# Where the sums of a two-level block product run: VectorE or GpSimd, and who stores the hidden features

## The chip, the cores and the metric

The kernel runs on one core of a Trainium2 chip. The metric is device time in microseconds of one execution; the time before is the median of three executions, 3026.63 us (3024.52 to 3027.03). The profiler recorded one further execution, of 3015.44 us, and its span from first to last instruction is 3013.7 us. Clock readings in this document (for example "at 882.9") are microseconds from the start of that span.

The engines are named as in the profile: PE (matrix products), DVE (VectorE), ACT (ScalarE), POOL (GpSimd) and SP, whose queue starts DMA transfers. Each engine works through its own queue in order.

## The reference, cut to what matters

A two-layer decoder trunk on 1024 tokens of width 1024: a mixer, a cross-attention and an MLP in each layer, each wrapped in two norms. Only the MLP is touched by the change, so it stands here alone:

```python
def _sq_relu_mlp(hn, w1, w2):
    return jnp.square(jax.nn.relu(hn @ w1)) @ w2

# in reference(), for each of 2 layers, after the mixer and the cross-attention
f = _sq_relu_mlp(_rmsnorm(h, g_ffn_pre[layer]), ffn_w1[layer], ffn_w2[layer])
h = h + _rmsnorm(f, g_ffn_post[layer])
```

The hidden width is 4096. All data is fp32.

## The kernel before, in words

**Products of fp32 in three parts.** Every fp32 operand is split into a high part (rounded by ACT, `split`, L137) and a low part (the remainder, on DVE, L143). A product then takes three matmuls: high by high, high by low, low by high (`prod`, L552 to L558). In the profile's rows `wh` and `wl` are the two parts of a weight or feature block, `hnh` and `hnl` those of the tokens.

**Seven products in place of eight.** The MLP's matrices are cut into 2 x 2 blocks, and a block product is made from seven smaller products by a Strassen-like scheme. The seven are numbered and run in the order `SEVEN = (1, 2, 6, 5, 7, 3, 4)`. Products 1 and 2 use blocks as they are, and so do 3 and 4 on one side; the others use sums of blocks. The hidden width is cut into eight groups (`GROUPS`), so *product (g, p)* is product p of group g: 24 matmuls of 128 x 128 by 128 x 512 each, in *up* (tokens by w1) as in *down* (hidden by w2).

**Up.** `up(g, p)` (L575) takes the next weight from a stream that makes weights up to three products ahead (`Stream`, its `ahead`). Making a weight means loading a block (`unit`, L474), forming its sum where the product needs one (`seven`, L479, four sums for each group, on POOL, rows of L489 in the profile), and splitting it. The tokens' blocks are made once for each layer: the last tiles of the cross-attention are normed, turned by PE (rows of `tp`) and copied by ACT into four blocks b11, b12, b21, b22 (`transpose_blocks`), and `sum_blocks` (L247) makes t2, t1, t3 and t4 from them and splits all of these and b22. It is one call, between `up(1, 1)` and `up(1, 2)`; four of its eight sums are on DVE (L260, L261) and four on POOL (L266, L272). Products 1 and 2 of groups 0 and 1 are run first, since they need no sum of the tokens, and the other ten products of these two groups after them.

**Evacuation.** Products 1, 6 and 5 are copied out of PSUM by ACT (`keep`, L587). Products 2, 7 and 3 go to `hidden` (L564): DVE adds the kept part (L571), then DVE makes the squared ReLU in one instruction (L572), and SP stores the result to DRAM (`hd`, L573). Product 4 has nothing to add: ACT makes the ReLU, DVE the square (L569). The same SP queue carries the loads of blocks.

**Down.** The first seven groups run in chunks (0, 1), (2, 3), (4, 5), (6). For product p both groups of a chunk follow each other: (0, 1), (1, 1), (0, 2), (1, 2), (0, 6) and so on. Both operands, the hidden blocks (read back from `hd`) and the blocks of w2, are made two products ahead: a block is loaded when a product first asks for it, so at p = 6 the load, two sums on each side (on POOL), and the splits all come in a row. Group 7 is done at the end without the scheme.

**What sets the order.** A scheduler puts each engine's instructions in an order by its own timeline; the order in which Python issues them sets priorities. Buffers (34 units of 4 KB a partition, 12 weight buffers, 3 raw ones) decide when a load can start.

Of the kernel before, what the change touches and what calls it, by code (L numbers as in the profile page):

```python
# [45 lines left out]
def half_cols(half):  # L46
    return slice(half * HALF, half * HALF + HALF)
# [30 lines left out]
class Trunk:  # L78
# [168 lines left out]
    def sum_blocks(self):  # L247

        nc, B, parts = self.nc, self.blocks, self.bparts
        sub, dve, pool = ALU.subtract, nc.vector, nc.gpsimd  # L250

        def part(name, xs, lo_eng="dve"):
            parts[name] = [self.parts([P, 2, HALF], "hn") for _ in range(2)]
            for w, x in zip(parts[name], xs):
                self.split(*w, x, lo_eng=lo_eng)

        b11, b12, b21, b22 = (B[n] for n in BLOCKS)
        t2 = [self.u([P, 2, HALF], F32, "blk") for _ in range(2)]
        for q in range(2):
            dve.tensor_tensor(b11[q], b12[q], b11[q], sub)  # L260
            dve.tensor_tensor(t2[q], b22[q], b11[q], sub)  # L261
        part("t2", t2)
        part("t1", b11)
        del B["11"], b11
        for q in range(2):
            pool.tensor_tensor(b12[q], b22[q], b12[q], sub)  # L266
        part("t3", b12)
        del B["12"], b12
        part("22", b22)
        del B["22"], b22  # L270
        for q in range(2):
            pool.tensor_tensor(b21[q], b21[q], t2[q], sub)  # L272
        del t2
        part("t4", b21)
        del B["21"], b21

    def norm_pre(self, h, gpre, hn=None):
# [200 lines left out]

    def seven(self, p, st, load, new, make, signs, eng):  # L479

# [46 lines left out]
    def up_weights(self, l):  # L527
        nc, st = self.nc, {}

        def make(gp):  # L530
# [4 lines left out]

            x = self.seven(p, st.setdefault(g, {}), load, lambda: self.wt([P, 2, HALF], F32, "sum"), None, 1, nc.gpsimd)
            w = self.parts([P, 2, HALF], "w", self.wt)
# [8 lines left out]
    def ffn(self, l):  # L546
# [13 lines left out]
        with self.psum(8, 0):  # L560
# [3 lines left out]
            def hidden(c, ps, g, b, q):  # L564

                x = self.t2()
                if c is None:
                    nc.scalar.activation(x, ps, AF.Relu)
                    nc.vector.tensor_tensor(x, x, x, ALU.mult)  # L569
                else:  # L570
                    nc.vector.tensor_tensor(x, c, ps, ALU.add)  # L571
                    nc.vector.scalar_tensor_tensor(x, x, 0.0, x, ALU.max, ALU.mult)  # L572
                nc.sync.dma_start(hd[g][BLOCKS.index(b), :, half_cols(q)], x)  # L573

            def up(g, p):  # L575
# [20 lines left out]
                for n in {2: ("b", 1), 7: (5,), 3: ("c", 6), 4: ("a",)}.get(p, ()):  # L596
                    del G[n]

            up(0, 1)
            self.flush(1)  # L600
            up(0, 2)
            self.flush()
            up(1, 1)
            self.sum_blocks()
            up(1, 2)
            for g in range(2):
                for p in SEVEN[2:]:
                    up(g, p)
            for g in range(2, GROUPS):
# [13 lines left out]

        sts = {}

        def make(gp):
            g, p = gp
            sa, sb = sts.setdefault(g, ({}, {}))
            res = []
            for st, load, sign in ((sa, hid(g), 1), (sb, second(g), -1)):  # L630
                x = self.seven(p, st, load, lambda: self.u([P, 2, HALF], F32, "blk"), None, sign, nc.gpsimd)
                w = self.parts([P, 2, HALF], "w", self.wt)
                self.split(*w, x)
                res.append(w)
            return res

        with self.psum(8, 0):
            W = Stream(self, [(g, p) for ch in CHUNKS for p in SEVEN for g in ch], 2, make=make)
            for ch in CHUNKS:
# [1286 lines left out]
```

## Time and profile before

| What | Value |
|---|---|
| median of 3 executions | 3026.63 us |
| the profiled execution, its span | 3015.44 us, 3013.7 us |
| mean granted PE clock | 0.977 |
| DVE, ACT, POOL busy, share of the span | 66%, 42%, 40% |
| up of layer 0, of layer 1, start of the first product | 870.86, 2331.51 |
| down of layer 0, of layer 1, start of the first product | 1208.79, 2669.91 |
| DMA moved | 385.09 MB, mean 128 GB/s |

How to read the rows that follow in the document. A row of the timeline has the start, the duration, the engine, the line of the kernel, the operation, what it writes and reads, and how many like it in a row (x); in square brackets stands how long the engine was idle before it and which instruction ended that. A row of the windows has a stretch of the span, its length, and for each engine the time in which it was busy and the number of instructions; behind them the granted PE clock, the DMA share and GB/s. A row of the waits has who waited for whom, the sum, the number of times and the longest. Where several instructions overlap at their ends, the durations of a row are a little longer than the distance between starts.

### The profile page before, as it was taken

The page shows a single profiled execution, that of the slowest core. Times are in us where ns is not written, and L with a number is a line of the kernel's source. Part 1 is how long each engine was busy: PE and PEld are TensorE (multiplying, and loading weights), DVE is VectorE, ACT ScalarE, POOL GpSimd, SP SyncE. Part 2 cuts the span into 40 slices and gives each one's busy share as a digit, 9 for nine tenths or more (in the row PEclk, how much of TensorE's full clock was granted, in tenths as well). Part 3 has the DMA queues.
Part 4 walks back from the last instruction along what each step waited for, and adds up shares of the span by engine and source line. Part 5 has one row for each costly group of instructions (what it writes and reads, how often), then busy time and mean ns, then how long its engine had stood idle before and what let it go on. Part 6 is the DMA issues. An engine that isn't in the chain of part 4 may idle for free. (4 is left out here: it accounts for less than half of the span.)

```text
span 3013.7 us, 38030 instructions
## 1 busy us (share of the span) xinstructions
PE 2843.7 (94%) x14470; PEld 2356.3 (78%) x14470; DVE 2000.8 (66%) x2372; ACT 1279.1 (42%) x2167; POOL 1205.0 (40%) x778
## 2 busy tenths in 40 slices
PE   7998999999998999799999998988999799989998
PEld 6787888787876888688867888987788588867886
DVE  5237778764367555599876657888634855548995
ACT  4445666543343323333345565553433333224332
POOL 2205544243344331776050113357433533347733
PEclk9999999999998999899999999999999899999999
DMA  4264444451322334432153346556223132253303
GB/s 164 103 179 131 156 155 146 137 187 42 117 102 85 101 110 151 164 111 85 64 203 109 117 144 193 182 171 237 84 91 112 67 111 103 105 207 108 105 28 140
DMA packets 165223, 385.09 MB, mean 128 GB/s; under 512 B 16748, under 2 KB 66316, under 8 KB 165040
## 3 DMA queue, kind: packets, MB, share of 16 engines
q1 hardware_dynamic: 165040, 382.66, 37.7%
q8 instruction: 114, 1.87, 0.3%
q14 instruction: 69, 0.57, 0.1%
HBM read 267.86 MB, written 113.69 MB: 127 GB/s over the span
## 5 line engine op out<-in xcount | busy, mean ns | idle before, releaser
L143 DVE TENSOR_TENSOR wl<-blk,wh 128x1024 fp32r<-128x1024 f32 x276 | 482.5, 1771 | 255.1 <-ACT wh L137 253.4
L489 POOL TENSOR_TENSOR blk<-blk 128x1024 f32<-128x1024 f32 x128 | 387.9, 3053 | 251.6 <-DMA blk<-hd 124.1
L137 ACT ACTIVATE wh<-blk 128x1024 fp32r<-128x1024 f32 x276 | 282.6, 1056 | 405.8 <-PE op L557 191.9
L556 PE MATMUL up<-hnh,wh 128*128 128x512 f32 x896 | 356.9, 399 | 16.3 <-ACT keep L587 9.2
L557 PE MATMUL up<-hnl,wh 128*128 128x512 f32 x896 | 356.9, 398 | 6.0 <-DVE hnl L143 6.0
L558 PE MATMUL up<-hnh,wl 128*128 128x512 f32 x896 | 354.6, 396 | 0.0
L556 PE MATMUL op<-wh 128*128 128x512 f32 x784 | 306.2, 394 | 27.5 <-ACT wh L137 27.5
L557 PE MATMUL op<-wl,wh 128*128 128x512 f32 x784 | 308.8, 394 | 4.8 <-DVE wl L143 4.7
L558 PE MATMUL op<-wh,wl 128*128 128x512 f32 x784 | 307.5, 392 | 0.0
L143 POOL TENSOR_TENSOR wl<-raw,wh 128x1024 fp32r<-128x1024 f32 x66 | 158.7, 2416 | 223.9 <-ACT wh L137 208.5
L137 ACT ACTIVATE wh<-raw 128x1024 fp32r<-128x1024 f32 (+1 forms) x163 | 170.6, 1058 | 129.8 <-DMA raw<-hd 25.4
L556 PEld LDWEIGHTS up<-hnh,wh 128*128 128x128 f32 x896 | 170.7, 191 | 59.3 <-ACT keep L587 10.7
L557 PEld LDWEIGHTS up<-hnl,wh 128*128 128x128 f32 x896 | 170.4, 190 | 46.2 <-DVE hnl L143 6.9
L558 PEld LDWEIGHTS up<-hnh,wl 128*128 128x128 f32 x896 | 169.8, 190 | 40.0
L143 DVE TENSOR_TENSOR wl<-raw,wh 128x1024 fp32r<-128x1024 f32 (+1 forms) x97 | 130.3, 1354 | 100.7 <-ACT wh L137 100.2
L556 PEld LDWEIGHTS op<-wh 128*128 128x128 f32 x784 | 148.8, 190 | 60.4 <-ACT wh L137 29.2
L187 POOL TENSOR_SCALAR st<-st 128x1 f32<-128x1 f32 x99 | 41.7, 421 | 358.8 <-ACT hn L299 306.6
L557 PEld LDWEIGHTS op<-wl,wh 128*128 128x128 f32 x784 | 149.0, 190 | 39.0 <-DVE wl L143 7.8
L489 POOL TENSOR_TENSOR sum<-blk 128x1024 f32<-128x1024 f32 x16 | 43.1, 2696 | 337.2 <-PE up L557 337.2
L558 PEld LDWEIGHTS op<-wh,wl 128*128 128x128 f32 x784 | 148.9, 190 | 30.4
L302 POOL TENSOR_TENSOR h<-h,hn 128x1024 f32<-128x1024 f32 x47 | 128.4, 2731 | 33.9 <-DVE hn L301 25.8
L587 ACT ACTIVATE keep<-up 128x512 f32<-128x512 f32 x96 | 56.7, 594 | 196.9 <-PE up L558 184.5
(439 smaller groups left out, 7200.0 us busy)
## 6 DMA issues: line engine op xcount, KB each, us to landing
blk<-in_ffn_w_dram SPq DMA_DIRECT2D x120, 512.0 KB, 3.9
h<-h SPq DMA_DIRECT2D x80, 512.0 KB, 4.0
hd<-t SPq DMA_DIRECT2D x128, 256.0 KB, 2.0
blk<-hd SPq DMA_DIRECT2D x56, 512.0 KB, 4.5
raw<-in_w_in_dram SPq DMA_DIRECT2D x24, 512.0 KB, 4.1
h<-in_x_dram SPq DMA_DIRECT2D x16, 512.0 KB, 7.0
raw<-in_xa_w_k_dram SPq DMA_DIRECT2D x16, 512.0 KB, 3.7
raw<-in_xa_w_v_dram SPq DMA_DIRECT2D x16, 512.0 KB, 3.9
```

The lines of the kernel that those rows point to most:

```text
L137: nc.scalar.activation(hi, src, AF.Copy)
L143: e.tensor_tensor(lo, src, hi.bitcast(F32), ALU.subtract)
L187: self.nc.gpsimd.tensor_scalar(dst, src, EPS, None, ALU.add)
L302: nc.gpsimd.tensor_tensor(h, h, t, ALU.add)
L489: eng.tensor_tensor(out, a, b, op)
L556: mm(ps, lh, rh, start=start and not i, stop=False, skip_group_check=True)
L557: mm(ps, lh, rl, start=False, stop=False, skip_group_check=True)
L558: mm(ps, ll, rh, start=False, stop=i == n - 1, skip_group_check=True)
L587: nc.scalar.activation(keep[:, q, :], ps, AF.Copy)
```

## The change

Five edits, all in the MLP:

1. In up, the four sums of weight blocks for each group move from POOL to DVE.
2. `sum_blocks` has all eight sums on DVE and becomes a generator of four steps: t2 and t1; t3; b22; t4. The first step is issued ahead of `up(1, 1)`, the second ahead of `up(1, 2)`, the others ahead of products 6 and 5 of group 0. The weight stream is two products ahead instead of three until `up(1, 2)` has been issued, then three.
3. `hidden` makes the squared ReLU on ACT in two instructions (ReLU, then Square) and stores it from ACT's own DMA queue. DVE keeps the add. For product 4 nothing is left on DVE.
4. In down, the blocks that the next product needs first are loaded one step earlier (`seq[n:n + 2]`).
5. In down, the sums of the first chunk (groups 0 and 1) move from POOL to DVE; the other chunks keep POOL.

```diff
     def sum_blocks(self):
...
-        sub, dve, pool = ALU.subtract, nc.vector, nc.gpsimd
+        tt = self.nc.vector.tensor_tensor
...
-            dve.tensor_tensor(b11[q], b12[q], b11[q], sub)
-            dve.tensor_tensor(t2[q], b22[q], b11[q], sub)
+            tt(b11[q], b12[q], b11[q], ALU.subtract)
+            tt(t2[q], b22[q], b11[q], ALU.subtract)
         part("t2", t2)
         part("t1", b11)
         del B["11"], b11
+        yield True
         for q in range(2):
-            pool.tensor_tensor(b12[q], b22[q], b12[q], sub)
+            tt(b12[q], b22[q], b12[q], ALU.subtract)
...
-            x = self.seven(p, st.setdefault(g, {}), load, lambda: self.wt([P, 2, HALF], F32, "sum"), None, 1, nc.gpsimd)
+            x = self.seven(p, st.setdefault(g, {}), load, lambda: self.wt([P, 2, HALF], F32, "sum"), 1, nc.vector)
...
                 x = self.t2()
-                if c is None:
-                    nc.scalar.activation(x, ps, AF.Relu)
-                    nc.vector.tensor_tensor(x, x, x, ALU.mult)
-                else:
+                if c is not None:
                     nc.vector.tensor_tensor(x, c, ps, ALU.add)
-                    nc.vector.scalar_tensor_tensor(x, x, 0.0, x, ALU.max, ALU.mult)
-                nc.sync.dma_start(hd[g][BLOCKS.index(b), :, half_cols(q)], x)
+                nc.scalar.activation(x, ps if c is None else x, AF.Relu)
+                nc.scalar.activation(x, x, AF.Square)
+                nc.scalar.dma_start(hd[g][BLOCKS.index(b), :, half_cols(q)], x)
...
+            W.ahead = 2
             up(0, 1)
             self.flush(1)
             up(0, 2)
             self.flush()
+            sums = self.sum_blocks()
+            next(sums)
             up(1, 1)
-            self.sum_blocks()
+            next(sums)
             up(1, 2)
+            W.ahead = 3
             for g in range(2):
                 for p in SEVEN[2:]:
+                    next(sums, None)
                     up(g, p)
...
+        seq = [(g, p) for ch in CHUNKS for p in SEVEN for g in ch]
+
+        def make(n):
+
+            for g, p in seq[n:n + 2]:
+                sa, sb = sts.setdefault(g, ({}, {}))
+                for st, load, more in ((sa, hid(g), {1: ("11",), 2: ("12",), 6: ("21", "22")}), (sb, second(g), {1: ("11",), 2: ("21",), 6: ("12", "22")})):
+                    for b in more.get(p, ()):
+                        if b not in st:
+                            st[b] = load(b)
...
-                x = self.seven(p, st, load, lambda: self.u([P, 2, HALF], F32, "blk"), None, sign, nc.gpsimd)
+                x = self.seven(p, st, load, lambda: self.u([P, 2, HALF], F32, "blk"), sign, nc.vector if g in CHUNKS[0] else nc.gpsimd)
```

How the instructions move is best seen at three places. A number behind a name tells one buffer from another; the two programs number differently.

**POOL where up begins, layer 0.** `h_8266` is the last token tile of the cross-attention, `st_8279` the norm factor of that tile; L489 is a sum of weight blocks. Before:

```order
L302 TENSOR_TENSOR h_8266<-h_8266,hn_8265 128x1024
L489 TENSOR_TENSOR sum_8346<-blk_8347,blk_8349 128x1024
L187 TENSOR_SCALAR st_8279<-st_8279 128x1
L489 TENSOR_TENSOR sum_8352<-sum_8346,blk_8232 128x1024
L489 TENSOR_TENSOR blk_8347<-blk_8232,blk_8347 128x1024
L188 TENSOR_TENSOR st_8279<-st_8279,mhalf_79 128x1
L489 TENSOR_TENSOR blk_8238<-blk_8238,sum_8352 128x1024
L266 TENSOR_TENSOR blk_8150<-blk_8159,blk_8150 128x1024
```

And now, with the first rows of down behind them:

```order
L306 TENSOR_TENSOR h_8266<-h_8266,hn_8265 128x1024
L187 TENSOR_SCALAR st_8279<-st_8279 128x1
L188 TENSOR_TENSOR st_8279<-st_8279,mhalf_79 128x1
L493 TENSOR_TENSOR blk_11141<-blk_11085,blk_11087 128x1024
L493 TENSOR_TENSOR blk_11143<-blk_11141,blk_10928 128x1024
```

The two small instructions of the norm have no sum ahead of them or between them any more, and POOL has nothing else in all of up.

**DVE where up's sums are made, layer 0.** `blk_7794` and `blk_7795` are the halves of b11, which become t1; t2 is `blk_8439`, `blk_8440` before and `blk_8396`, `blk_8397` now; `hnl` is a low part of a token block, `wl` of a weight. Before:

```order
L143 TENSOR_TENSOR wl_8530<-blk_8238,wh_8529 128x1024
L260 TENSOR_TENSOR blk_7794<-blk_8150,blk_7794 128x1024
L260 TENSOR_TENSOR blk_7795<-blk_8151,blk_7795 128x1024
L261 TENSOR_TENSOR blk_8439<-blk_8159,blk_7794 128x1024
L261 TENSOR_TENSOR blk_8440<-blk_8160,blk_7795 128x1024
L143 TENSOR_TENSOR wl_8561<-blk_8349,wh_8560 128x1024
L143 TENSOR_TENSOR hnl_8446<-blk_8439,hnh_8445 128x1024
L571 TENSOR_TENSOR t2_8508<-keep_8412,up_8494 128x512
L143 TENSOR_TENSOR hnl_8448<-blk_8440,hnh_8447 128x1024
```

Now the part from the first of these sums to the first low half of t2 reads:

```order
L260 TENSOR_TENSOR blk_7794<-blk_8150,blk_7794 128x1024
L260 TENSOR_TENSOR blk_7795<-blk_8151,blk_7795 128x1024
L143 TENSOR_TENSOR wl_8470<-sum_8418,wh_8469 128x1024
L143 TENSOR_TENSOR wl_8519<-blk_8419,wh_8518 128x1024
L261 TENSOR_TENSOR blk_8396<-blk_8159,blk_7794 128x1024
L267 TENSOR_TENSOR blk_8150<-blk_8159,blk_8150 128x1024
L261 TENSOR_TENSOR blk_8397<-blk_8160,blk_7795 128x1024
L267 TENSOR_TENSOR blk_8151<-blk_8160,blk_8151 128x1024
L143 TENSOR_TENSOR wl_8524<-blk_8238,wh_8523 128x1024
L143 TENSOR_TENSOR wl_8565<-blk_8421,wh_8564 128x1024
L275 TENSOR_TENSOR blk_7811<-blk_7811,blk_8396 128x1024
L143 TENSOR_TENSOR hnl_8403<-blk_8396,hnh_8402 128x1024
```

Ahead of these twelve now stand, in this order, the last tile's norm (L287), the split of the weight of (1, 2), the four sums of group 0's weights with two adds of `hidden` among them, and one more split: eight instructions from the split of (1, 2) on. So twenty instructions run from that split to the first low half of t2, and the second low half comes three further on.

**DVE where down begins, layer 0.** `acc` is the output's accumulator, `op` a PSUM bank. Before, with all sums on POOL:

```order
L143 TENSOR_TENSOR wl_10484<-blk_10481,wh_10483 128x1024
L143 TENSOR_TENSOR wl_10490<-blk_10487,wh_10489 128x1024
L658 TENSOR_TENSOR acc_10517<-acc_10517,op_10529 128x512
L658 TENSOR_TENSOR acc_10520<-acc_10520,op_10530 128x512
L658 TENSOR_TENSOR acc_10523<-acc_10523,op_10531 128x512
L143 TENSOR_TENSOR wl_10542<-blk_10539,wh_10541 128x1024
L658 TENSOR_TENSOR acc_10526<-acc_10526,op_10532 128x512
L143 TENSOR_TENSOR wl_10554<-blk_10549,wh_10553 128x1024
```

Now, from the sixth instruction behind the same two splits (there named `wl_10542` and `wl_10546`) to the last split of (0, 6); the five ahead of it are sums:

```order
L143 TENSOR_TENSOR wl_10602<-blk_10599,wh_10601 128x1024
L493 TENSOR_TENSOR blk_10607<-blk_10539,blk_10605 128x1024
L493 TENSOR_TENSOR blk_10637<-blk_10589,blk_10591 128x1024
L493 TENSOR_TENSOR blk_10537<-blk_10539,blk_10537 128x1024
L673 TENSOR_TENSOR acc_10573<-acc_10573,op_10585 128x512
L673 TENSOR_TENSOR acc_10576<-acc_10576,op_10586 128x512
L673 TENSOR_TENSOR acc_10579<-acc_10579,op_10587 128x512
L493 TENSOR_TENSOR blk_10487<-blk_10487,blk_10607 128x1024
L673 TENSOR_TENSOR acc_10582<-acc_10582,op_10588 128x512
L143 TENSOR_TENSOR wl_10610<-blk_10607,wh_10609 128x1024
```

Behind them follow four sums, a split, three sums and the split `wl_10650` that product (1, 6) needs. All sixteen sums of the first chunk are in DVE's queue among the splits, and the adds to `acc`, which wait for PE, stand among them.

More of the change, by code (lines that the diff above doesn't have):

```diff
@@ L247, in sum_blocks, with part @@
     def sum_blocks(self):
-        nc, B, parts = self.nc, self.blocks, self.bparts
-        sub, dve, pool = ALU.subtract, nc.vector, nc.gpsimd
-        def part(name, xs, lo_eng="dve"):
+        B, parts = self.blocks, self.bparts
+        tt = self.nc.vector.tensor_tensor
+        def part(name, xs):
             parts[name] = [self.parts([P, 2, HALF], "hn") for _ in range(2)]
             for w, x in zip(parts[name], xs):
-                self.split(*w, x, lo_eng=lo_eng)
+                self.split(*w, x)
         b11, b12, b21, b22 = (B[n] for n in BLOCKS)
@@ L264, in sum_blocks @@
         del B["11"], b11
+        yield True
         for q in range(2):
-            pool.tensor_tensor(b12[q], b22[q], b12[q], sub)
+            tt(b12[q], b22[q], b12[q], ALU.subtract)
         part("t3", b12)
         del B["12"], b12
+        yield True
         part("22", b22)
         del B["22"], b22
+        yield True
         for q in range(2):
-            pool.tensor_tensor(b21[q], b21[q], t2[q], sub)
+            tt(b21[q], b21[q], t2[q], ALU.subtract)
         del t2
@@ L275, in sum_blocks @@
         del B["21"], b21
+        yield True
     def norm_pre(self, h, gpre, hn=None):
@@ L477, in unit, with seven @@
         return t
-    def seven(self, p, st, load, new, make, signs, eng):
+    def seven(self, p, st, load, new, signs, eng):
         sub, add = ALU.subtract, ALU.add
@@ L624, in ffn @@
         sts = {}
-        def make(gp):
-            g, p = gp
-            sa, sb = sts.setdefault(g, ({}, {}))
+        seq = [(g, p) for ch in CHUNKS for p in SEVEN for g in ch]
[6 more added lines that the diff above has]
+                            st[b] = load(b)
+            g, p = seq[n]
+            sa, sb = sts[g]
             res = []
             for st, load, sign in ((sa, hid(g), 1), (sb, second(g), -1)):
-                x = self.seven(p, st, load, lambda: self.u([P, 2, HALF], F32, "blk"), None, sign, nc.gpsimd)
+                x = self.seven(p, st, load, lambda: self.u([P, 2, HALF], F32, "blk"), sign, nc.vector if g in CHUNKS[0] else nc.gpsimd)
                 w = self.parts([P, 2, HALF], "w", self.wt)
@@ L637, in ffn @@
         with self.psum(8, 0):
-            W = Stream(self, [(g, p) for ch in CHUNKS for p in SEVEN for g in ch], 2, make=make)
+            W = Stream(self, range(len(seq)), 2, make=make)
             for ch in CHUNKS:
```

## The prediction, made blind

> **What bounds the kernel now.** I read the page's first part, then the waits of PE, then windows over the MLP, and last the timelines of the engines around PE's idle times.
>
> ```profile
> PE 2843.7 (94%) x14470; PEld 2356.3 (78%) x14470; DVE 2000.8 (66%) x2372; ACT 1279.1 (42%) x2167; POOL 1205.0 (40%) x778
> ```
>
> PE is busy for 94% of the span, so an edit that moves work between the other engines can gain only where PE waits. The waits of PE between 840 and 1500, the MLP of layer 0, show where:
>
> ```profile
> PE op L556 <- ACT wh L137: 13.8, 2, 11.3
> PE tp L239 <- ACT wh L137: 7.4, 1, 7.4
> PE up L556 <- ACT keep L587: 4.6, 1, 4.6
> PE up L557 <- DVE hnl L143: 3.0, 1, 3.0
> PE up L556 <- ACT wh L137: 3.0, 1, 3.0
> PE op L557 <- DVE wl L143: 2.4, 2, 2.1
> ```
>
> A table of windows says what these cost. Its rows are the first nine products of up, the rest of up, the first six products of down and the 42 after them, then both starts in layer 1.
>
> ```profile
> 870.86:946.75 75.89, 57.85 (x233) 45.23 (x231) 64.37 (x45) 32.35 (x48) 46.88 (x19) 0.84 0.17 57
> 946.75:1208.79 262.04, 262.04 (x1133) 212.32 (x1132) 148.40 (x142) 79.24 (x101) 68.39 (x24) 1.00 0.35 121
> 1208.79:1262.59 53.80, 37.61 (x145) 29.41 (x144) 22.52 (x15) 15.68 (x20) 41.48 (x16) 0.84 0.48 177
> 1262.59:1491.07 228.48, 228.48 (x1009) 189.20 (x1008) 213.85 (x175) 91.19 (x95) 129.41 (x40) 1.00 0.24 78
> 2331.51:2407.77 76.26, 57.28 (x234) 45.12 (x231) 64.65 (x45) 32.12 (x48) 46.88 (x19) 0.87 0.16 57
> 2669.91:2723.53 53.62, 37.57 (x146) 29.29 (x145) 22.33 (x15) 15.69 (x20) 41.70 (x16) 0.84 0.49 179
> ```
>
> Past the starts PE is busy in every microsecond at full clock: 262.04 / 47 = 5.575 us for a product of up (0.232 a matmul), 228.48 / 42 = 5.44 for one of down (0.227). Nothing can be gained there. At the starts, nine products of up and two turns of token tiles (0.8 each) should take 51.8, and take 75.89: 24.1 lost, 24.5 in layer 1. Six products of down should take 32.6: 21.2 lost, 21.0 in layer 1. So **90.8 us** is all that this change can win. The idle time itself is 34.2 in a layer; the rest is a low clock (0.84 to 0.87) and slow matmuls behind it.
>
> **Up's start, part by part.** Timelines of POOL, DVE and PE around the first idle time:
>
> ```profile
> 872.56 0.21 POOL L187 TENSOR_SCALAR st<-st 128x1 f32<-128x1 f32 x1 [0.16 <-ACT hn L281]
> 872.86 0.56 POOL L188 TENSOR_TENSOR st<-st,mhalf 128x1 f32<-128x1 f32 x1
> 873.79 3.37 POOL L302 TENSOR_TENSOR h<-h,hn 128x1024 f32<-128x1024 f32 x1 [0.38 <-DVE hn L301]
> 877.12 3.38 POOL L489 TENSOR_TENSOR sum<-blk 128x1024 f32<-128x1024 f32 x1
> 880.58 0.22 POOL L187 TENSOR_SCALAR st<-st 128x1 f32<-128x1 f32 x1
> 880.88 2.40 POOL L489 TENSOR_TENSOR sum<-sum,blk 128x1024 f32<-128x1024 f32 x1
> 883.25 2.36 POOL L489 TENSOR_TENSOR blk<-blk 128x1024 f32<-128x1024 f32 x1
> 885.55 1.56 POOL L188 TENSOR_TENSOR st<-st,mhalf 128x1 f32<-128x1 f32 x1
> ```
>
> ```profile
> 887.15 3.35 DVE L283 SCALAR_TENSOR_TENSOR hn<-h,st,gain 128x1024 f32<-128x1024 f32 x1 [0.46 <-POOL st L188]
> 896.23 2.35 DVE L260 TENSOR_TENSOR blk<-blk 128x1024 f32<-128x1024 f32 x2
> ```
>
> ```profile
> 877.20 1.07 ACT L281 ACTIVATE hn<-h 128x1024 f32<-128x1024 f32 x1 [2.68 <-POOL h L302]
> 890.65 1.94 PE L239 MATMUL tp<-c_ident,hn 128*128 128x128 f32 x8 [7.37 <-ACT wh L137]
> ```
>
> The view puts the 7.37 down to a split, but the turn reads `hn`, which DVE ended at 890.5, because the norm factor of the last tile was stuck between sums on POOL. With the sums gone, the factor follows ACT's square: 878.4 + 0.9 (as at 872.56), DVE about 1.2, so 880.5. PE ends (0, 2) at 877.44 + 5.57 = 883.0, and this wait is **gone**. What is late next is t2. PE goes on with the turn, (1, 1) and (1, 2) and is through at 883.0 + 0.8 + 11.15 = 894.9. Product (0, 6) then needs t2's low halves, behind twenty instructions of DVE.
>
> ```profile
> 877.19 0.32 SPq L303 DMA_DIRECT2D h<-h  x1
> blk<-in_ffn_w_dram SPq DMA_DIRECT2D x120, 512.0 KB, 3.9
> L137 ACT ACTIVATE wh<-blk 128x1024 fp32r<-128x1024 f32 x276 | 282.6, 1056 | 405.8 <-PE op L557 191.9 <-PE up L557 82.5 <-POOL blk L489 81.4
> ```
>
> The first of the twenty splits the weight of (1, 2), whose load, made one product later now, sits on SP's queue behind the store of the last tile: 877.5 + 3.9 + 1.06 for ACT = 882.5. Eighteen of the twenty are of 128x1024; with POOL empty I take 2.35 / 2 = 1.18 each (the pair at 896.23), and two adds at 0.69 (the row at 1229.47 below). That is 22.6, so the first low half is there at 905.1 and the second, three on, at 908.6. PE does four high-by-high matmuls (0.9), which its new order puts first, meanwhile. It is idle for 905.1 - 894.9 - 0.9 = 9.3, works off twelve matmuls, and is idle 0.7 more. I add 1.5 for slow matmuls behind the idle time, from the turn that took 1.94 instead of 1.04. Loss 11.5 where it was 24.1: **12.6 won**. The bounds of one DVE sum are 1.18 and, if POOL shared the time with it as at 873.79, 3.4; POOL has no work there, so I take 1.18. From t3 on DVE leads PE by some 3 us for each product, so I cost the later waits (hnl 3.0, wh 3.0, keep 4.6) at nothing.
>
> **Down's start.** SP, POOL, ACT, DVE and PE, each from its timeline:
>
> ```profile
> 1198.82 13.25 SPq L573 DMA_DIRECT2D hd<-t  x6
> 1212.16 0.88 SPq L476 DMA_DIRECT2D blk<-hd  x2
> ```
>
> ```profile
> 1217.70 41.80 POOL L489 TENSOR_TENSOR blk<-blk 128x1024 f32<-128x1024 f32 x16 [53.03 <-DMA blk<-hd]
> 1214.26 2.01 ACT L137 ACTIVATE wh<-blk 128x1024 fp32r<-128x1024 f32 x2 [3.92 <-issue]
> 1215.36 2.36 DVE L143 TENSOR_TENSOR wl<-blk,wh 128x1024 fp32r<-128x1024 f32 x2 [3.64 <-ACT wh L137]
> 1229.47 0.69 DVE L658 TENSOR_TENSOR acc<-acc,op 128x512 f32<-128x512 f32 x1 [0.67 <-PE op L558]
> 1233.26 1.20 PE L556 MATMUL op<-wh 128*128 128x512 f32 x4 [2.54 <-ACT wh L137]
> 1254.96 2.08 PE L556 MATMUL op<-wh 128*128 128x512 f32 x4 [11.26 <-ACT wh L137]
> ```
>
> The loads for p = 6 stood behind six stores on SP, and the sixteen sums then took POOL 41.8. The stores leave SP, so the loads go out when buffers come free, and the inputs are there before 1217. That alone gains nothing: the sums now follow two splits that wait for the weight buffers of (0, 1), and end at 1217.7 as before. Nine instructions of 1.18 bring 1228.3; the third add waits for PE until 1230.2; a sum, an add and a split bring 1233.2. PE ended (1, 2) at 1230.6 and did four matmuls: idle 1.7. It ends (0, 6) at 1233.2 + 20 x 0.227 = 1237.7. Six further (7.1) and ACT's split give (1, 6) its operand at 1241.4: idle 3.7. PE does four matmuls, then waits for ACT's two splits of (0, 5) until 1243.5 (idle 1.2), does four more, and the rest of both, 40 matmuls, ends at 1253.5. Seven products without a wait would end at 1246.9: loss 6.6, with 1.5 for the clock 8.1, where it was 21.2. **13.1 won**. From there DVE leads again. The chunks behind keep POOL; I cost the earlier loads at nothing, since PE never waited there.
>
> **ACT and the stores.** In up's steady part ACT is busy 79.24 in 47 products, so 11.8 in a group of seven (39.0).
>
> ```profile
> L393 ACT ACTIVATE t<-t 128x512 f32<-128x512 f32 x40 | 25.0, 629 | 68.6 <-DVE t L392 68.5
> L571 DVE TENSOR_TENSOR t<-keep,up 128x512 f32<-128x512 f32 x96 | 65.2, 680 | 33.1 <-PE up L558 33.0
> hd<-t SPq DMA_DIRECT2D x128, 256.0 KB, 2.0
> ```
>
> A group adds eight squares and six ReLUs of 0.63, 8.8 in all, and eight stores. The trace shows no store issued by ACT; the bounds are nothing and SP's time to landing, 2.0, and I take 0.32, SP's issue. That makes 23.2 of 39.0: hidden under PE. The copies that free PSUM wait behind a ReLU for at most the two adds of a product (0.68 each), and PE comes back to a bank a whole product later. DVE loses six squares and two multiplies in a group and gains four sums, hidden too. A microsecond that is not hidden here counts fourteen times in a run (seven later groups, two layers).
>
> **The sum.** 12.6 + 13.1 = 25.7 a layer, 51.4 in two layers, so about 52: the profiled execution goes from 3015.4 to 2963, and the median, which lies 11.2 above it, from 3026.6 to **2975**.
>
> **What the Trainium skill adds.** The POOL sum at 873.79 and DVE's norm at 887.15 take 3.4 where 2.36 and 1.2 would do, so the two engines exclude each other. The Trainium skill, "SBUF — State Buffer", section "Who interferes with whom", says that a DVE instruction with two SBUF inputs contends with a GpSimd one that reads SBUF; the trace agrees (3.35). "Perfetto Trace Analysis" in the Trainium skill, section "Optimizing Scalar/DVE Operations", warns for this reason that moving work between those two might not help; rival A gives its time. The Trainium skill, "TensorE: Matmul & The Clock Gate", section "What's actually happening", lets the clock fall after an idle window of about 3.4 us. By that rule the four 1.5s would go, an estimate of 2969. The trace does not quite agree: four matmuls took 1.20 after 2.54 of idle, where 3 x 0.227 + 0.39 = 1.07 is usual.
>
> **The rivals.** *A: DVE gains nothing on POOL.* If each moved sum held DVE for POOL's 2.36, seven of up's twenty and sixteen of down's would cost 1.18 more each: 8.3 and 18.9 a layer, 27 against 25.7 won, so 3028, no change. Against it: the pair at 896.23. *B: the starts close almost whole*, because DVE begins earlier than I think or its rows overlap better: up to 80 won, 2940 to 2954. *C: a new wait in up's steady part*, ACT's splits or copies queued behind a ReLU that waits for a DVE add: 2 us a group are 28, so 3003; I put it at 3000 to 3020. For it: every add waits for PE; against it, PE returns a product later. *D: slower.* If ACT is held x us by each store, it has 39.0 - 20.6 = 18.4 for eight, so from x = 2.3 ACT becomes the bound, and from 2.8 (14 x 8 x 0.46 = 52) the kernel is slower than before; x = 3.1 would give 3065. Landing took 2.0, so a store that held ACT until it had landed comes close; SP's 0.32 speaks against it.
>
> **How the numbers follow.** Forecast 0.76 (2954 to 3000, from DVE sums a quarter dearer to idle times half as long), A 0.04, B 0.07, C 0.09, D 0.04. The range 2954 to 3004 takes the near half of C in and holds 0.80. Faster by over 0.2%, about what a measurement of this kernel can tell from no change: 0.92; within it 0.04; slower 0.04.
>
> **What would show it.** Right: the 7.4 before the turn is gone; PE waits for `hnl` of t2 some 9 us near 895; at down's start three waits of 1 to 4 us in place of 11.3; DVE's sums at 1.2; PE busy throughout the rest of up. Wrong: PE waits in up past 950 (C or D, by whether ACT is busy or waits), DVE's sums near 2.4 (A), or no wait for t2 (B).

## The result, and the profile after

The changed kernel takes **2978.39 us** (median of 4 runs, 2974.45 to 2981.21) where the kernel before took 3025.57 on the same chip (median of 4, 3022.73 to 3027.03): a ratio of 0.9844, with a 95% interval of 0.9827 to 0.9861. The forecast was 2975.0. The profiled execution took 2979.67, 35.8 less than that of before; the medians are 47.2 apart.

First the engines' busy time, from the page of the changed kernel, and the row of the page on the stores (their queue, how many, KB each, median us from issue to landing):

```profile
PE 2846.6 (96%) x14470; PEld 2355.4 (79%) x14470; DVE 1909.4 (64%) x2348; ACT 1402.7 (47%) x2391; POOL 898.2 (30%) x674
hd<-t ACTq DMA_DIRECT2D x128, 256.0 KB, 2.9
```

PE is busy as long as before (2843.7); what went is time around its work. POOL lost 307 us of work. DVE, which took over the sums, is busy for 91 us less: it lost the squares, and it no longer shares its time with POOL in the stretches where POOL is now idle. Now the waits of PE from 840 to 1500, the whole MLP of layer 0:

```profile
PE op L561 <- DVE wl L143: 4.8, 6, 1.4
PE op L560 <- ACT wh L137: 3.1, 1, 3.1
PE up L560 <- ACT hnh L137: 2.5, 1, 2.5
PE up L560 <- DVE blk L267: 2.5, 1, 2.5
PE up L561 <- DVE hnl L143: 2.4, 1, 2.4
```

34.2 us of waiting have become 15.3. The 11.3 and the 7.4 are gone. But the first row is new in kind: six waits for `wl` in down, of which five lie far behind its start. The windows of the changed kernel, with the columns as before: up's start, up's steady part and down's start in layer 0, then the chunk of groups 4 and 5 (sixteen products of down, the 25th to the 40th), then the two starts in layer 1.

```profile
877.51:940.34 62.83, 55.45 (x236) 43.65 (x235) 50.73 (x48) 39.32 (x63) 5.73 (x7) 0.92 0.22 75
940.34:1201.98 261.64, 261.64 (x1129) 211.79 (x1128) 109.58 (x110) 131.30 (x195) 0.00 (x0) 1.00 0.36 129
1201.98:1242.50 40.52, 36.01 (x145) 28.60 (x144) 34.00 (x32) 17.73 (x24) 0.00 (x0) 0.92 0.65 225
1340.42:1433.04 92.62, 89.19 (x385) 71.54 (x384) 89.80 (x70) 33.96 (x35) 57.06 (x18) 1.00 0.18 57
2318.35:2380.82 62.47, 55.38 (x236) 43.64 (x235) 50.73 (x48) 40.01 (x64) 5.74 (x7) 0.92 0.22 75
2642.26:2682.85 40.59, 36.09 (x145) 28.63 (x144) 34.00 (x32) 17.73 (x23) 0.00 (x0) 0.92 0.67 221
```

From here on **U** is up's start (from the first product to the tenth), **D** down's start (from the first to the seventh), **K** the chunk of groups 4 and 5. One correction first: the prediction's windows for U end two or three matmuls early (233 and 234 of 236). Counted alike, U was 76.6 and 76.7 before.

| layer 0, layer 1 | before | after | won |
|---|---|---|---|
| U | 76.6, 76.7 | 62.8, 62.5 | 13.8, 14.3 |
| D | 53.8, 53.6 | 40.5, 40.6 | 13.3, 13.0 |
| K | 87.0, 87.5 | 92.6, 92.7 | -5.6, -5.2 |

The starts won 54.3 and the chunk gave back 10.8, so 43.5 remain, between the 35.8 of the profiled pair and the 47.2 of the medians. The profiled executions also differ where nothing was changed: over the first 600 us the granted clock was 0.95 and 0.97 in this one against 0.98 and 0.98, and its first product of up starts 6.7 later (877.51 against 870.86).

What stands at the starts now? Up's start in the changed kernel, POOL, DVE, ACT and PE, each from its timeline:

```profile
885.41 0.57 POOL L188 TENSOR_TENSOR st<-st,mhalf 128x1 f32<-128x1 f32 x1
...
886.01 1.29 DVE L287 SCALAR_TENSOR_TENSOR hn<-h,st,gain 128x1024 f32<-128x1024 f32 x1 [4.43 <-POOL st L188]
889.67 1.23 DVE L143 TENSOR_TENSOR wl<-blk,wh 128x1024 fp32r<-128x1024 f32 x1 [2.37 <-ACT wh L137]
...
902.22 1.22 DVE L261 TENSOR_TENSOR blk<-blk 128x1024 f32<-128x1024 f32 x1
...
910.17 1.22 DVE L143 TENSOR_TENSOR hnl<-blk,hnh 128x1024 fp32r<-128x1024 f32 x1
```

```profile
903.47 1.06 ACT L137 ACTIVATE hnh<-blk 128x1024 fp32r<-128x1024 f32 x1 [2.13 <-DVE blk L261]
...
904.58 0.73 PE L560 MATMUL up<-hnh,wh 128*128 128x512 f32 x2 [2.47 <-DVE blk L267]
907.80 1.22 PE L560 MATMUL up<-hnh,wh 128*128 128x512 f32 x2 [2.49 <-ACT hnh L137]
911.44 0.79 PE L561 MATMUL up<-hnl,wh 128*128 128x512 f32 x1 [2.42 <-DVE hnl L143]
```

The norm factor is ready at 886, the turn waits for nothing, and PE waits three times for t2: for the first high half (the view names DVE's L267, but ACT's split, which ends at 904.53, is what the matmul of 904.58 reads), for the second, and for the first low half, ready at 911.4. From 889.67 on DVE has not a gap in its work. Down's start, DVE and PE:

```profile
1208.51 2.36 DVE L143 TENSOR_TENSOR wl<-blk,wh 128x1024 fp32r<-128x1024 f32 x2 [3.65 <-ACT wh L137]
1210.79 5.88 DVE L493 TENSOR_TENSOR blk<-blk 128x1024 f32<-128x1024 f32 x5
...
1226.21 0.50 PE L561 MATMUL op<-wl,wh 128*128 128x512 f32 x1 [1.38 <-DVE wl L143]
...
1234.17 1.22 PE L560 MATMUL op<-wh 128*128 128x512 f32 x2 [3.13 <-ACT wh L137]
```

The sums take DVE 1.14 to 1.22 each, and two waits, 1.4 and 3.1, have taken the place of the 11.3. The place that nobody had asked about is the third one, POOL in the chunk of groups 4 and 5:

```profile
1326.47 2.40 POOL L493 TENSOR_TENSOR blk<-blk 128x1024 f32<-128x1024 f32 x1 [18.70 <-DVE wl L143]
1330.10 35.95 POOL L493 TENSOR_TENSOR blk<-blk 128x1024 f32<-128x1024 f32 x11 [1.23 <-DVE wl L143]
```

POOL runs eleven sums without a pause; the first of PE's waits for `wl` comes at 1363.85.

### The profile page after: what moved, and what is told of

The parts are those of the page before. It is cut to its first block, busy times and chain, and to the rows that moved or that the text cites. A ratio compares the mean times of both kernels' runs of the same rounds, so it can differ in the third digit from the quotient of the medians.

```text
span 2977.9 us, 37928 instructions
## 1 busy us (share of the span) xinstructions
PE 2846.6 (96%) x14470; PEld 2355.4 (79%) x14470; DVE 1909.4 (64%) x2348; ACT 1402.7 (47%) x2391; POOL 898.2 (30%) x674
## 5 line engine op out<-in xcount | busy, mean ns | idle before, releaser
L143 DVE TENSOR_TENSOR wl<-blk,wh 128x1024 fp32r<-128x1024 f32 x276 | 451.7, 1659 | 320.0 <-ACT wh L137 320.0
L493 POOL TENSOR_TENSOR blk<-blk 128x1024 f32<-128x1024 f32 x80 | 252.4, 3183 | 869.0 <-DVE wl L143 863.5
L673 DVE TENSOR_TENSOR acc<-acc,op 128x512 f32<-128x512 f32 x192 | 123.8, 676 | 4.3 <-PE op L562 4.1
L287 DVE SCALAR_TENSOR_TENSOR hn<-h,st,gain 128x1024 f32<-128x1024 f32 x48 | 101.8, 2122 | 26.1 <-POOL st L188 24.8
```

Of the source, the lines that this page charges most:

```text
L143: e.tensor_tensor(lo, src, hi.bitcast(F32), ALU.subtract)
L287: nc.vector.scalar_tensor_tensor(hn, h, st[:, 1:2], gpre, ALU.mult, ALU.mult)
L493: eng.tensor_tensor(out, a, b, op)
L673: nc.vector.tensor_tensor(dst, dst, ps[i], ALU.add)
```

## The experiments

Twelve kernels, each made from the changed one. The ratio is that of the runs to the runs of before on the same chip, with its 95% interval; stretches are from the profiled execution, layer 0 and layer 1. Kernels with the same code in up have U from 61.8 to 63.4 in layer 0 and from 62.1 to 62.7 in layer 1, and those with the same code in down have D from 39.4 to 40.8. So a difference of up to 1.6 in U of layer 0, 0.6 in U of layer 1 or 1.4 in D says nothing by itself.

| kernel | U | D | K | median us | ratio |
|---|---|---|---|---|---|
| changed | 62.8, 62.5 | 40.5, 40.6 | 92.6, 92.7 | 2978.39 | 0.9844 (0.9827 to 0.9861) |
| late_loads | 63.0, 62.5 | 45.4, 45.2 | 87.0, 87.4 | 2976.50 | 0.9853 (0.9827 to 0.9878) |
| all_dve | 63.4, 62.3 | 40.8, 40.3 | 87.0, 87.0 | 2969.08 | 0.9815 (0.9797 to 0.9832) |
| chunk0_pool | 63.1, 62.7 | 45.0, 44.8 | 92.8, 92.5 | 2990.60 | 0.9886 (0.9872 to 0.9901) |
| store_sp | 63.5, 63.3 | 39.4, 39.6 | 92.7, 92.9 | 2980.66 | 0.9858 (0.9842 to 0.9875) |
| down_before | 61.8, 62.1 | 48.9, 47.7 | 87.0, 87.6 | 2987.86 | 0.9882 (0.9859 to 0.9905) |
| up_sums_pool | 64.1, 64.1 | 39.5, 40.6 | 92.7, 92.6 | 2981.18 | 0.9856 (0.9841 to 0.9871) |
| sums_pool_3ahead | 63.8, 63.8 | 39.4, 40.8 | 92.7, 92.8 | 2981.17 | 0.9858 (0.9844 to 0.9873) |
| up_all_pool | 71.2, 67.9 | 39.6, 39.6 | 92.6, 92.7 | 2998.18 | 0.9917 (0.9903 to 0.9932) |
| one_step | 63.5, 62.9 | 39.5, 40.4 | 92.7, 92.7 | 2975.02 | 0.9841 (0.9824 to 0.9857) |
| squares_dve | 64.5, 65.4 | 40.3, 40.4 | 92.6, 92.6 | 2987.67 | 0.9880 (0.9864 to 0.9896) |
| three_groups | other order | 41.8, 43.4 | 87.0, 87.0 | 2975.64 | 0.9840 (0.9825 to 0.9855) |
| three_groups_b | other order | 42.4, 42.3 | 87.0, 87.0 | 2965.47 | 0.9812 (0.9795 to 0.9828) |

Two of the expectations below give D of the changed kernel in layer 1 as 42.2, or say that records are missing there: that was a miscount, and the window above has it whole, 40.6. U of before stands in them by the prediction's shorter window.

### The chunk that got slower: late_loads and all_dve

late_loads undoes edit 4:

```diff
-            for g, p in seq[n:n + 2]:
-                sa, sb = sts.setdefault(g, ({}, {}))
...
-                            st[b] = load(b)
             g, p = seq[n]
-            sa, sb = sts[g]
+            sa, sb = sts.setdefault(g, ({}, {}))
```

> Edit 4 alone is undone: down loads a block when a product first asks for it; the rest stays as changed. Measured on stretches of the profile: K, from the start of down's 25th product to the start of its 41st (the chunk of groups 4 and 5), was 87.0 before and is 92.6 in layer 0 and 92.3 in layer 1 of the changed kernel; D, from down's first product to its seventh, was 53.8 and 53.6 and is 40.5 and 42.2. Theory: the earlier loads let POOL form the sums of the chunk in one bunch (eleven without a pause at 1330.10), and DVE's splits beside it take two to three times their time, so PE waits for the low parts. Then K goes back to 87 to 88 in both layers, D stays within 2 of what it is, and the time falls by about 11, to 2967. Rival 1: the bunch comes from edit 5, since POOL is free earlier; then K stays at 92 and the time at 2978. Rival 2: the earlier loads are what shortens the start; then D goes up by 4 or more a layer, and the time to 2986 or more.

all_dve extends edit 5:

```diff
-sign, nc.vector if g in CHUNKS[0] else nc.gpsimd)
+sign, nc.vector)
```

> Edit 5 extended: the sums of all chunks of down are on DVE, POOL does none. Theory (contention of POOL and DVE): without POOL beside it, DVE's splits of two go from 2.8 or more each back to 1.2, which pays for sixteen more sums of 1.14 a chunk; K falls to 87 to 89, D stays, and the time is about 2967 to 2970. Rival: DVE, busy in 30.0 of 30 us between 1330 and 1360 already, becomes the bound with 18 us more a chunk; K stays above 92, the chunk of groups 2 and 3 (87.0 now) gets waits too, and the time is 2985 or more.

K went back to 87 in both. So it is the early loads together with POOL's sums: taking away either one is enough. Edit 5 has no part in it: chunk0_pool, which undoes it, keeps K at 92.8 and 92.5. How that works is read from the groups of instructions inside K in four kernels (count, busy time and mean ns of one, then the idle time before them). Before:

```profile
L489 POOL TENSOR_TENSOR blk<-blk 128x1024 f32<-128x1024 f32 x16 | 52.6, 3311 | 12.5 <-DVE wl L143 8.1 <-DMA blk<-hd 2.7 <-DMA blk<-in_ffn_w_dram 1.4
L143 DVE TENSOR_TENSOR wl<-blk,wh 128x1024 fp32r<-128x1024 f32 x33 | 60.5, 1864 | 3.1 <-ACT wh L137 3.1
L143 DVE TENSOR_TENSOR wl<-raw,wh 128x1024 fp32r<-128x1024 f32 x2 | 3.5, 1728 | 1.8 <-ACT wh L137 1.8
```

The changed kernel, DVE and POOL:

```profile
L143 DVE TENSOR_TENSOR wl<-blk,wh 128x1024 fp32r<-128x1024 f32 x33 | 67.0, 2063 | 1.0 <-ACT wh L137 1.0
L493 POOL TENSOR_TENSOR blk<-blk 128x1024 f32<-128x1024 f32 x18 | 58.2, 3259 | 9.6 <-DVE wl L143 8.2 <-issue 1.2
```

Without the early loads:

```profile
L143 DVE TENSOR_TENSOR wl<-blk,wh 128x1024 fp32r<-128x1024 f32 x33 | 60.6, 1867 | 2.7 <-ACT wh L137 2.7
L493 POOL TENSOR_TENSOR blk<-blk 128x1024 f32<-128x1024 f32 x16 | 52.3, 3298 | 12.7 <-DVE wl L143 8.1 <-DMA blk<-hd 3.1 <-DMA blk<-in_ffn_w_dram 1.3
```

All sums on DVE:

```profile
L143 DVE TENSOR_TENSOR wl<-blk,wh 128x1024 fp32r<-128x1024 f32 x32 | 38.4, 1220 | 7.3 <-ACT wh L137 7.3
L493 DVE TENSOR_TENSOR blk<-blk 128x1024 f32<-128x1024 f32 x18 | 21.5, 1218 | 0.0
```

A split takes DVE 1.22 when POOL is silent and 1.86 on average beside POOL's sums. Before, DVE had 3.1 + 1.8 = 4.9 us to spare in these 87: PE did not wait, but the cover was thin. With its inputs there earlier, POOL no longer pauses for a DMA, so eighteen sums instead of sixteen fall into K. The same 33 splits take 6.5 us longer (67.0 - 60.5). DVE cannot use up all of the 4.9: it still idles 2.8 in the changed kernel (92.62 - 89.80). So most of the 6.5 reaches PE, which loses 5.6: five waits of 3.4 in all, and a slower start of the matmuls behind each. With the eighteen sums on DVE their 21.5 us are paid for by the splits (67.0 - 38.4 = 28.6), and 7 us are to spare again.

late_loads was half a surprise all the same: D rose by 4.8 and 4.6, as its second rival had it, so edit 4 wins at the start about what it loses in the chunk, and the median fell by 2 where 11 were expected. DVE's queue in late_loads shows why D rose:

```profile
1204.79 3.61 DVE L493 TENSOR_TENSOR blk<-blk 128x1024 f32<-128x1024 f32 x3
1213.96 0.69 DVE L667 TENSOR_TENSOR acc<-acc,op 128x512 f32<-128x512 f32 x1 [5.55 <-PE op L562]
```

The other sums stand behind an add that waits 5.55 for PE; with the early loads the scheduler puts eight sums ahead of that add.

### Down's start: chunk0_pool, store_sp, down_before

chunk0_pool undoes edit 5 (`nc.vector if g in CHUNKS[0] else nc.gpsimd` becomes `nc.gpsimd`).

> Edit 5 alone is undone: the sums of down's first chunk are on POOL again, with the loads still one step early. By the prediction the sixteen sums on POOL (41.8 in a row) are what made PE wait at down's start: D, 40.5 and 42.2 now, goes to 50 or more in both layers, and the time up by about 20 to 26, to 2998 to 3005. Rival: the stores on SP's queue were the cause and the early loads cure it; then D stays under 45 and the time under 2988. K (92.6 and 92.3) stays if the early loads make it, as the theory says, and falls to 88 or less if POOL's free first chunk makes it.

store_sp takes the queue alone out of edit 3:

```diff
-                nc.scalar.dma_start(hd[g][BLOCKS.index(b), :, half_cols(q)], x)
+                nc.sync.dma_start(hd[g][BLOCKS.index(b), :, half_cols(q)], x)
```

> Of edit 3 the queue alone is undone: squares on ACT, stores from SP's queue. Theory: the last stores wait on SP until 1205 or so, and the loads for p = 6, at 1200.24 to 1203.48 now, go out behind them, land near 1210 to 1213, just when DVE's sums begin (1210.79): D up by 0 to 2, U and K unchanged, time 2978 to 2983. Rival: the stores' queue is what made the start late (as the six stores of 13.25 before down suggest), D goes up by 4 or more a layer and the time to 2986 or more.

down_before undoes edits 4 and 5 together, by the two edits of late_loads and chunk0_pool.

> Edits 4 and 5 both undone, so that down is as before but for the stores, which stay on ACT's queue. Each of the two alone, undone, cost 4.5 to 4.8 a layer at down's start (D 45.3 without the early loads, 45.0 with the sums on POOL), together they and the stores won 13.3. Theory: POOL's sixteen sums in a row (41.8 to 45.4) end last, and they begin when the loads land; behind SP's stores that was 8.9 after down's first product, with early loads 5.6 ahead of it; with late loads but no stores in their way, it is from 1 to 5 after it, so D is 46 to 51, and 3 to 7 of the gain belong to the stores' queue. The time is 2984 to 2998, K 87 to 88. Rival: as the prediction had it, the stores' queue gains nothing alone, POOL begins as late as before and D is 53 or more.

With the sums on POOL and the loads early D rose by 4.5 and 4.2 only, not by 13: a miss for the prediction's account. In store_sp D did not rise at all. In down_before it rose by 8.3 and 7.1, so 4.9 and 5.9 of the gain stay with nothing of down changed but the stores' queue, as that theory had it. (The edits of up are in this kernel too; one with them, the stores on SP and the rest of down as before was not run.) POOL's sums in chunk0_pool (down starts at 1201.95) and then in down_before (it starts at 1199.49):

```profile
1197.83 45.39 POOL L493 TENSOR_TENSOR blk<-blk 128x1024 f32<-128x1024 f32 x16 [312.21 <-DMA blk<-hd]
```

```profile
1198.28 44.74 POOL L493 TENSOR_TENSOR blk<-blk 128x1024 f32<-128x1024 f32 x16 [313.83 <-DMA blk<-hd]
```

Before, POOL began 8.9 behind down's first product (1217.70 against 1208.79); now it begins 4.1 and 1.2 ahead of it (the 5.6 in the expectation of down_before should read 4.1, and its 1 to 5 behind down's first product came out as 1.2 ahead). The sixteen sums still take 45, but they begin 13.0 and 10.1 sooner. With the stores back on SP, its queue and DVE in store_sp (down starts at 1199.79):

```profile
1190.24 14.49 SPq L575 DMA_DIRECT2D hd<-t  x6
1204.82 0.89 SPq L480 DMA_DIRECT2D blk<-hd  x2
```

```profile
1208.60 2.48 DVE L493 TENSOR_TENSOR blk<-blk 128x1024 f32<-128x1024 f32 x2
```

The loads for p = 6 go out at 1204.82, behind six stores, and still land in time, because DVE begins its sums 8.8 behind down's start in either case (1208.60; 1210.79 in the changed kernel): it has two splits to do first. So the three edits overlap. Each makes up for part of what another leaves, and none of them carries the 13 alone.

### Up's start: which part of edits 1 to 3

up_sums_pool undoes edit 1 (`nc.vector` in `up_weights` becomes `nc.gpsimd`).

> Edit 1 alone is undone: up's four sums of weight blocks for each group are on POOL again, while the tokens' sums stay on DVE in four steps. U, from up's first product to its tenth, was 75.9 and 76.3 before and is 62.8 and 62.5. Theory: DVE loses four of the twenty instructions that stand before the first low half of t2 (4.6), but each sum of 2.36 on POOL keeps DVE from SBUF meanwhile (9.4 for four); U goes to 65 to 70 and the time up by 6 to 14, to about 2988. The wait of 7 us before the last token turn does not come back, because the stream of weights, now only two products ahead, has POOL form the norm factor first. Rival 1: the wait comes back with the sums (the prediction's step on the norm factor was about edit 1); then U is 70 or more and the time 2993 or more. Rival 2: edit 1 does nothing for the start and the order of the tokens' sums all; U stays within 1.5 and the time at 2978.

sums_pool_3ahead does the same and takes out both lines that set `W.ahead`, so that the stream of weights is three products ahead from the start.

> Edit 1 undone and, of edit 2, the stream of weights three products ahead from the start, as before; the tokens' sums stay on DVE in four steps. With the sums alone on POOL U was 63.9 and 64.1 (62.8 and 62.5 in the changed kernel). Theory: it is the stream's depth, not the engine, that keeps the norm factor of the last tile from its turn; with three products ahead POOL does three sums of weights between its two instructions again, PE waits some 7 us before the last token turn in each layer, and since these us cover part of the wait for t2, U goes to 66 to 72, the time up by 5 to 16 over the 2981 of sums on POOL alone, to 2986 to 2997. Rival: the four steps of the tokens' sums hide it, U stays under 65.5 and the time under 2984.

Neither came to much. U rose by 1.3 and 1.6 with the weight sums on POOL, less than the theory had (1.3 is within the spread of layer 0), and did not move further with the deeper stream, although the wait came back. PE's waits from 840 to 945 in sums_pool_3ahead:

```profile
PE tp L239 <- DVE hn L287: 7.4, 1, 7.4
PE up L560 <- ACT wh L137: 0.6, 1, 0.6
PE up L560 <- ACT keep L589: 0.4, 1, 0.4
PE up L561 <- DVE hnl L143: 0.4, 1, 0.4
```

The 7.4 before the last turn stands **in place of** the three waits for t2, not on top of them: what sets the end is the chain to t2's halves, and PE waits for it either at the turn or at (0, 6). So, with the other edits in place, taking away the wait before the turn was worth nothing by itself. Three more parts were left:

up_all_pool undoes edit 1 and the engine of edit 2:

```diff
-            tt(b12[q], b22[q], b12[q], ALU.subtract)
+            self.nc.gpsimd.tensor_tensor(b12[q], b22[q], b12[q], ALU.subtract)
...
-            tt(b21[q], b21[q], t2[q], ALU.subtract)
+            self.nc.gpsimd.tensor_tensor(b21[q], b21[q], t2[q], ALU.subtract)
```

> Edit 1 undone and, of edit 2, the engine: the sums for t3 and t4 are on POOL again beside the sums of weights; the four steps, the stream of two ahead, edits 3 to 5 stay. So far neither the weight sums on DVE (U 62.8 to 63.9 without) nor the wait before the turn (U 63.8 with it) explains the 13 won at up's start. Theory: it is POOL's queue, with the sums for t3 and t4 behind those of the weights at 2.4 to 3.4 each, beside which DVE is slow; PE waits at products 5 to 7 again as before (hnl 3.0, wh 3.0, keep 4.6), and U goes to 70 to 76 in both layers, time 2990 to 3004. Rival: the four steps, or the squares that left DVE, make the gain; U stays at 62 to 66 and the time under 2986.

one_step undoes the steps of edit 2:

```diff
-            sums = self.sum_blocks()
-            next(sums)
             up(1, 1)
-            next(sums)
+            for _ in self.sum_blocks():
+                pass
             up(1, 2)
```

> Of edit 2 the steps alone are undone: all eight sums of the tokens on DVE, in one call between (1, 1) and (1, 2) as before. Theory: the scheduler puts DVE's rows in nearly the same order with one call, so the steps are worth little: U within 1.5 of 62.8 and 62.5, time within 3 of 2978. Rival: the steps are what brings t2 early; U is 66 or more and the time 2985 or more.

squares_dve undoes edit 3 as a whole (squares on DVE, stores from SP).

> Edit 3 alone is undone: DVE makes the squared ReLU in one instruction, SP's queue stores; the rest stays as changed. By the prediction the squares on ACT are hidden and win nothing past the starts: the steady part of up, 261.6 and 261.4 now, stays within 1. At up's start DVE has two squares more in each of (0, 2) and (1, 2), ahead of t2's low halves: U up by 1 to 3. At down's start the loads stand behind the last stores on SP again, though asked for one step early: D, 40.5 (and 40.6 in layer 1, where seven matmul records are missing) goes up by 1 to 5. Time 2982 to 2994. Rival 1: nothing depends on edit 3, U and D stay within 0.7, time 2976 to 2980. Rival 2: DVE, with sums and squares both, becomes the bound in up's steady part, which grows by 5 or more.

The steps are worth nothing that shows. The squares are worth 1.7 and 3.0 in U, of which the 1.7 is hardly beyond the spread; D of squares_dve did not rise, where 1 to 5 were expected. The sums on POOL are worth 8.4 and 5.5; the 5.5 of layer 1 lies under what that theory had asked for, and the waits did not come where it put them: PE waits 9.6 for t2's high halves and 4.5 for low halves, and not at all for `wh` or `keep`. DVE in up_all_pool, with POOL's sums beside it:

```profile
897.03 2.35 DVE L260 TENSOR_TENSOR blk<-blk 128x1024 f32<-128x1024 f32 x2
899.30 3.40 DVE L261 TENSOR_TENSOR blk<-blk 128x1024 f32<-128x1024 f32 x1
902.62 3.38 DVE L143 TENSOR_TENSOR wl<-sum,wh 128x1024 fp32r<-128x1024 f32 x1
905.92 3.36 DVE L261 TENSOR_TENSOR blk<-blk 128x1024 f32<-128x1024 f32 x1
```

Where POOL pauses, a sum takes 1.18 (2.35 for two); beside POOL's sums for t3 and t4 the same instruction takes 3.4. The two sums of t2 alone lose 4.3 that way. Edit 1 did little alone because in up_sums_pool POOL's four sums were over at 893.8, before t2's began.

### Two tries for a better version

all_dve is one: K is 5.6 shorter in each layer, and nothing else is longer. For up's start, three_groups also runs products 1 and 2 of group 2 ahead of (0, 6), on top of all_dve, so that DVE has 11 us more for t2.

```diff
             up(1, 2)
+            up(2, 1)
+            up(2, 2)
             W.ahead = 3
-            for g in range(2):
+            for g in range(3):
```

> A version to beat both: all sums of down on DVE, and products 1 and 2 of group 2 run ahead of (0, 6) as well, which need no sum of the tokens and give DVE and ACT 11 us more for t2. Theory: what is left at up's start is DVE's work ahead of t2; the three waits of 2.2 to 2.5 at (0, 6) go, and with them the slow matmuls behind; up as a whole (its first product to down's first), 325.1 and 323.7 with all sums on DVE, goes to 313 to 316 (56 products of 5.575 and two turns are 313.8), the time by about 21 under that kernel's 2969, to 2945 to 2952. Rival: the two further products hold blocks and buffers that the stream needs, or their loads come late; PE waits at (2, 1), (2, 2) or past (0, 6), up stays at 319 or more and the time above 2958.

The rival came true. ACT in three_groups, where `wh` at 899.93 is the weight of (2, 1):

```profile
894.21 2.96 ACT L137 ACTIVATE hnh<-blk 128x1024 fp32r<-128x1024 f32 x3 [1.21 <-DVE blk L261]
897.08 1.06 ACT L589 ACTIVATE keep<-up 128x512 f32<-128x512 f32 x2
898.03 2.00 ACT L137 ACTIVATE hnh<-blk 128x1024 fp32r<-128x1024 f32 x2
899.93 1.05 ACT L137 ACTIVATE wh<-blk 128x1024 fp32r<-128x1024 f32 x1
```

That weight stands behind six splits of the tokens (one more at 891.94), and PE waits 6.4 for it and the next. three_groups_b asks for these weights before the tokens' sums:

```diff
             self.flush()
+            W.fill(6)
             sums = self.sum_blocks()
```

> The version with three groups ahead of (0, 6) and all sums of down on DVE, with the weights of (2, 1) and (2, 2) asked for before the tokens' sums, since ACT made the first of them only behind six splits of the tokens. Theory: the waits of 4.0 and 2.4 for these weights go and no wait for t2 comes in their place; up as a whole (its first product to down's first), 323.5 and 325.0 there, goes to 313 to 317, the time by 14 to 22 to 2954 to 2962. Rival: DVE and ACT are the bound whatever the order, since the two weights' splits and copies stand ahead of t2 now; then PE waits at (0, 6), up stays at 320 or more and the time above 2968.

Half of what was expected: up as a whole takes 319.7 and 319.3, against 325.1 and 323.7 in all_dve, and one wait of 3.0 for t2's low half is left; at down's start 1.5 and 2.0 are given back. Its median, 2965.47, is the lowest of all, and its ratio lies within the interval of all_dve's. Both are below the changed kernel's, with intervals that overlap its own a little; that they are faster rests on the stretches, K above all, more than on the totals.

## Why the prediction was right in its sum

**The size.** 51.4 were forecast for the starts, 54.3 came. 10.8 of it went in K, which the prediction had at nothing, and the median ended 3.4 above the forecast, well inside the range. That it came so near is in part luck: by the stretches 43.5 of the 51.4 were won, while executions of the changed kernel alone lie between 2974 and 2981.

**The step that failed** is the last sentence on down: "The chunks behind keep POOL; I cost the earlier loads at nothing, since PE never waited there." That PE does not wait says that there is cover, not how much. DVE had 4.9 us of it in 87 and could use only about half, and the earlier loads, by letting POOL run on, made its splits 6.5 longer: PE lost 5.6. late_loads and all_dve show both halves of it. Without this wait the median would be near 2968, under the forecast but in the range.

**Up's start: the times were right, the reason partly not.** The first low half of t2 was forecast for 905.1; it ended at 911.4, and that is 904.7 when the later start of this execution (6.7) is taken off. 11.5 were to be lost, 11.0 were (62.8 - 51.8). DVE's sums took 1.22, not the 2.36 of rival A. But of the loss the view shows 7.4 as idle and the rest, 3.6, as slow matmuls, where 10 and 1.5 were forecast. The sign that it named, one wait of some 9 for `hnl`, did not show: two of the three waits, 5.0 of the 7.4, are for t2's high halves, which the prediction took to be there in time. And the prediction tells the gain as that of a wait that goes; sums_pool_3ahead has that wait and loses 1.0 and 1.3. The gain is made of POOL's silence beside DVE (8.4 and 5.5) and of the squares (1.7 and 3.0). That leaves 3.7 and 5.8 of U's 13.8 and 14.3, which come only when several parts go together; that was not divided further, nor was the engine of t3 and t4 tried without edit 1.

**Down's start: the same.** 13.1 were forecast, 13.3 and 13.0 came; waits of 1.7, 3.7 and 1.2 were forecast, 1.4 and 3.1 came; the sums were to begin 8.9 behind down's start and began 8.8 behind it. But "that alone gains nothing", said of the loads that go out sooner, is false: with the sums left on POOL and up's edits in place, moving the stores won 5 to 6 and the early loads some 3 to 4 more. With the sums on DVE it holds for the stores (store_sp), not for the early loads, whose place in DVE's order is worth 4.6 to 4.8.

**Two readings on slow matmuls were wrong.** The 1.20 for four matmuls behind 2.54 of idle was no sign of a lower clock: the granted clock from 1233.26 to 1234.46 of before is 1.00, and it falls at 1234.69. And the estimate of 2969 does not follow from the prediction's own waits, since two of them, 9.3 and 3.7, are longer than the 3.4 that it goes by.

**ACT and the stores** were right. In up's steady part ACT went from 79.24 to 131.30, so by 7.8 in a group where 8.8 were forecast, stores apart; up's steady part takes 261.64 and the same stretch of before, counted alike, 261.35. There is no new wait in it (rivals C and D). The rows of ACT's queue put 0.33 on each store, the value taken from SP's 0.32, and ACT can work on meanwhile: the split at 893.87 takes 1.04 as usual across the store at 893.99.

## What to carry to other kernels

A stretch in which the busiest engine never waits can still be nearly full: before calling an earlier transfer free, add up the idle time of the engine *next* to the bottleneck there, and ask which third engine the transfer sets free to run. Two waits one behind the other on the same chain are one wait: taking away the first moves it to the second, and the gain has to be looked for in what feeds the chain. Where several edits aim at one wait, each undone alone tells only what the others leave to it.

## What the runs showed of the hardware

**A sum on POOL slows both engines.** Alone a 128x1024 sum takes POOL 2.40 (at 880.88 before) and DVE 1.22; together POOL takes 3.26 to 3.31 on average in K and DVE up to 3.4. So the eighteen sums on DVE cost less than they save there: 21.5 against 28.6 in K. The Trainium skill, "SBUF — State Buffer", section "Who interferes with whom", calls the ports that the two share an exclusive lock; these rows agree.

**The clock halves behind waits of only 2.5 to 3.1 us.** The mean of 0.92 at both starts of the changed kernel is made of one stretch at half clock in each, with 1.00 around it (the columns are PE alone, the granted clock and DMA):

```profile
905.39:915.63 10.24, 5.41 (x12) 0.50 0.16 53
1233.07:1239.89 6.82, 5.71 (x13) 0.50 0.57 181
```

The first begins behind the wait of 2.47 that ends at 904.58, the second inside the wait of 3.13 that ends at 1234.17. The two matmuls at 907.80 and at 1234.17, at half clock, took 1.22 each time; those at 904.58, still at full clock, took 0.73, and two without a wait take 0.62 (0.23 + 0.39), so a wait costs 0.1 even without the clock. The slow matmuls cost 3.6 at up's start and 3.4 at down's (40.5 - 32.6, less 4.5 idle), twice the 1.5 that was forecast. The Trainium skill, "TensorE: Matmul & The Clock Gate", section "What's actually happening", puts the window behind which the clock falls at about 3.4 us; no single wait here was that long, so the measurement decides against reading that figure as a safe length for one wait.
